# Seven-product feed-forward: one PSUM tile per partial sum, products in an order that a small list scheduler writes, weight parts six products ahead

## The chip, the cores and the metric

The kernel runs on one core of a Trainium2 chip. The metric is device time in microseconds (us) of one execution. TensorE (PE in the rows, its weight loads PEld) multiplies, VectorE (DVE) and ScalarE (ACT) prepare operands and drain PSUM, SyncE (SP) issues the weight loads. Before the change the time is 3714.63 us, the median of three runs (3712.78 to 3716.22).

## The reference: what is computed

Two models run one after the other on 512 tokens of width 1024. The second is a two-layer network on 528 tokens (512 and 16 meta tokens), each layer a feed-forward, a mixer and another feed-forward. The change touches only the second model's four feed-forwards:

```
def swiglu(x, w_gate, w_up, w_down):
    return (jax.nn.silu(x @ w_gate) * (x @ w_up)) @ w_down

h = h + 0.5 * swiglu(rmsnorm(h, norm_gains[l, 0]), ffn_w_gate[l, 0], ffn_w_up[l, 0], ffn_w_down[l, 0])
h = h + mixer(...)
h = h + 0.5 * swiglu(rmsnorm(h, norm_gains[l, 2]), ffn_w_gate[l, 1], ffn_w_up[l, 1], ffn_w_down[l, 1])
```

`w_gate` and `w_up` are 1024 x 2816, `w_down` is 2816 x 1024, all float32. The last feed-forward drops the meta tokens and works on 512.

## The kernel before, in words

**Operands in two parts.** Each float32 operand is split into a high part (ScalarE copy to the rounded type, `whi`) and a low part (VectorE subtraction, `wlo`), in `wsplit` (L212 to L214) and `split` (L216). A product is then three matmuls: high by high, high by low, low by high. Weights come in pieces of 128 x 512 (`raw`, loaded by SyncE at L197 or L1016). The tiles rotate through a fixed number of buffers, `WB` at L51: 6 raw, 3 sum, 9 whi, 9 wlo. These rings serve the whole kernel.

**One feed-forward** (`ffn2`, L1087) has 22 hidden blocks of 128 columns. Block `m` needs a gate and an up column block. Seven of the blocks (`DIRECT`, L53: 0, 3, 7, 11, 15, 18, 21) are done directly: 48 matmuls into one PSUM tile for gate, 48 for up. The others are done as a pair by seven half-size products in place of eight (`strassen`, L1051): gate weights have halves `a`, `b` along the contraction, up weights `c`, `d`; the tokens have halves `a`, `b`. The parts are `a`, `b`, `d` and four sums s1 = c + d, s2 = s1 - a, s3 = a - c, s4 = b - s2 (`pair`, L1007). On the token side `form` (L317) makes two matching combinations, `f1` and `f2`, from four pairs of row blocks. A product (`prod`, L1041) is 12 matmuls of 264 columns (256 in the last feed-forward). The first feed-forward does blocks 0 to 2 directly, so that there are 13 + 3 x 15 = 58 pairs in all.

**PSUM.** In this part of the kernel a pool `psP` has three tiles of two banks each and `psS` two tiles of one bank. A pair takes one `psP` tile `yx` that holds two sums, Y in its first bank and X in its second, and one tile `z`. Y is not cleared between products: `a`, `s2`, `s3`, `d` accumulate on it one after another, and it is copied out between them by ScalarE (L1064, L1069, L1075). X and Z are added by VectorE (L1062).

**The order.** The products of a pair go to TensorE as: `a`, `b` | `s2` | `s1`, `s3` | `d` | `s4`. The generator is stepped by hand (L1141 to L1147) so that the previous pair's `d` comes between `b` and `s2`, and its `s4` between `s2` and `s1`. TensorE keeps that order (`pinned`, L225). All seven parts of a pair are written ahead of the pair before it (`ahead`, L1124), as far as buffers let them. The framework's scheduler sets the order on the other engines at build time, earlier code first among what it holds ready; at run time each engine works through its own list in order.

**Rounds.** After blocks 7, 15 and 21 (`ROUNDS`, L52) the blocks so far are multiplied by their rows of `w_down`: eight outputs (`dn`), each a sum over the round's 8 or 6 blocks. `act` (L1112) makes a block's hidden value: scale, silu, product, split. Before that, at the start of a feed-forward, `stats` and `stats2` compute the norm factor `rb`, and `forms` the last of the token combinations.

Of the kernel before, what the change touches and what calls it, by code (L numbers as in the profile page):

```python
# [16 lines left out]
AF = mybir.ActivationFunctionType  # L17
# [43 lines left out]
class Net:  # L61
    def __init__(self, ctx, tc, d):
        nc = self.nc = tc.nc
        self.tc = tc
        self.d = d
        self.n = 0
        self.xp = ctx.enter_context(tc.tile_pool(name="xp", bufs=1))
        self.cp = ctx.enter_context(tc.tile_pool(name="cp", bufs=1))
        self.sp = ctx.enter_context(tc.tile_pool(name="sp", bufs=NSLOT))
        self.mp = ctx.enter_context(tc.tile_pool(name="mp", bufs=24))  # L70
        self.qp = ctx.enter_context(tc.tile_pool(name="qp", bufs=8))
        self.wp = ctx.enter_context(tc.tile_pool(name="wp", bufs=4))
# [5 lines left out]
        self.pinned = False  # L78

        self.cst = self.cp.tile([128, 144], F32, name="cst")  # L80
# [129 lines left out]
        return w[c // WU][:, c % WU : c % WU + n]  # L210

    def wsplit(self, raw, hi, lo, c):  # L212
        self.nc.scalar.activation(hi[:, c], raw[:, c], AF.Copy)  # L213
        self.nc.vector.tensor_tensor(out=lo[:, c], in0=raw[:, c], in1=hi[:, c], op=ALU.subtract)  # L214

    def split(self, a, name):  # L216
        nc = self.nc
# [786 lines left out]
    def c2(self, l, off):  # L1004
        return lambda k: self.v2[:, l * V2 + off + k : l * V2 + off + k + 1]

    def pair(self, gsrc, usrc):  # L1007


        nc = self.nc  # L1010
        C = slice(0, WU)
        raw = []
        for src in (gsrc, usrc):
            for h in range(2):
                raw.append(self.wtile("raw"))
                nc.sync.dma_start(raw[-1], src[:, WU * h : WU * h + WU])  # L1016
        a, b, c, d = raw

        def parts(t):
            h, l = self.wtile("whi"), self.wtile("wlo")  # L1020
            self.wsplit(t, h, l, C)
            return h, l

        def sum_(i, j, op=ALU.subtract):
            t = self.wtile("sum")
            nc.vector.tensor_tensor(out=t, in0=i, in1=j, op=op)
            return t

        w = {"a": parts(a), "b": parts(b)}
        s1 = sum_(c, d, ALU.add)  # L1030
        s2 = sum_(s1, a)
        w["s2"] = parts(s2)
        s3 = sum_(a, c)
        w["s1"] = parts(s1)
        s4 = sum_(b, s2)
        w["s3"] = parts(s3)
        w["d"] = parts(d)
        w["s4"] = parts(s4)
        return w

    def prod(self, o, w, xs, c, first):  # L1041

# [5 lines left out]
                    stop=k == NK // 2 - 1 and i == 2, skip_group_check=not first,  # L1048
                )

    def strassen(self, w, xs, T, rb, act):  # L1051


        nc = self.nc
        h = T // 2
        a, b = slice(0, h), slice(h, T)
        x1, x2 = xs[: NK // 2], xs[NK // 2 :]
        f1, f2 = zip(*self.forms)
        pa = self.P("yx")
# [3 lines left out]
        self.prod(Y, w["a"], x1, a, True)  # L1063
        nc.scalar.copy(s[:, a], Y)  # L1064
        self.prod(X, w["b"], x2, a, True)
        tt(s[:, a], X, s[:, a], ALU.add)
        yield
        self.prod(Y, w["s2"], f2, a, False)
        nc.scalar.copy(s[:, b], Y)  # L1069
        yield  # L1070
        pz = self.P("z")
        Z = pz[:, 0, :h]
        self.prod(Z, w["s1"], f1, a, True)
        self.prod(Y, w["s3"], f1, b, False)
        nc.scalar.copy(u[:, b], Y)  # L1075
        tt(u[:, b], Z, u[:, b], ALU.add)
        yield
        self.prod(Y, w["d"], f2, b, False)
        tt(u[:, b], u[:, b], rb[:, b], ALU.mult)
        tt(u[:, a], Y, rb[:, a], ALU.mult)  # L1080
        yield
        self.prod(Z, w["s4"], x2, b, False)
        tt(s[:, b], Z, s[:, b], ALU.add)
        act(s, u, True)
        yield

    def ffn2(self, l, f, xs, g, next_g, out=None):  # L1087
        nc, d = self.nc, self.d
        T = NX if (l, f) == (L - 1, 1) else T2
        self.psum(2)  # L1090
        gw, uw, dw = d["ffn_g"][l, f], d["ffn_u"][l, f], d["ffn_d"][l, f]
        acts = []
        srcs = [w for m in range(NF) for w in (gw[m], uw[m])]
        done = []
        if (l, f) == (0, 0):
# [13 lines left out]
                    nc.scalar.copy(t[:, :T], p[1])  # L1109
                    done.append(t[:, :T])  # L1110

        def act(s, u, scale):  # L1112
# [4 lines left out]
            acts.append(self.split(s[:, :T], "fa"))  # L1117

        pend = iter(())
        new = []  # L1120
        seven = lambda m: m < NF and not (m in DIRECT or done[2 * m : 2 * m + 2])
        wp = {}

        def ahead(m):  # L1124

            if m not in wp and seven(m):
                wp[m] = self.pair(srcs[2 * m], srcs[2 * m + 1])

        def forms():
            for k in range(len(self.forms), NK // 2):  # L1130
                self.form(k, T, g)

        if done:
            forms()
        for m in range(NF):
            ahead(m)
            self.pinned = m > 0
            if seven(m):
                if seven(m + 1) and m + 1 not in ROUNDS:
                    ahead(m + 1)  # L1140
                cur = self.strassen(wp.pop(m), xs, T, rb, act)  # L1141
                next(cur)
                next(pend, None)
                next(cur)
                next(pend, None)
                next(cur)
                pend = cur  # L1147
            else:
                ps = done[2 * m : 2 * m + 2]
                o = 2 * m + len(ps)  # L1150
                if m == 0 and not ps:
# [5 lines left out]
                for i in range(o, 2 * m + 2):  # L1157
                    if len(ps) == 2:
                        break
                    p = self.outs(1, T, "gu")  # L1160
                    self.group([srcs[i]], xs, T, p)
                    ps.append(p[0][1])
                    for _ in pend:
                        pass
                act(self.mul_r(ps[0], rb, "fg"), self.mul_r(ps[1], rb, "fu"), False)
            if m + 1 in ROUNDS:
                for _ in pend:
                    pass
                o = m + 1 - len(acts)
                fin = m == NF - 1  # L1170
                if fin:
                    self.forms = self.next_forms
                dsrc = lambda i: dw[i][:, 128 * o : 128 * m + 128]
                for i in range(NK - 1 if fin and out is not None else NK):
                    p = self.outs(1, T, "dn")[0]
                    self.down(dsrc(i), acts, T, p)
                    xv = self.xt[i][:, :T]
                    nc.vector.scalar_tensor_tensor(
                        out=xv, in0=p[1], scalar=0.5, in1=xv, op0=ALU.mult, op1=ALU.add
                    )  # L1180
                    if fin:
                        new.append(self.finish(i, T, next_g))
                if fin and out is not None:
                    self.ending(out, self.wload(dsrc(NK - 1)), acts)
                acts.clear()
        self.pinned = False
        return new

    def ending(self, out, ws, acts):
# [776 lines left out]
```

## Time and profile before

| what | value |
|---|---|
| median of three runs | 3714.63 us |
| profiled execution, its own time | 3718.47 us |
| span of its instructions | 3716.7 us |
| TensorE matmul busy | 3544.7 us, 95% |
| weight load busy | 3146.8 us, 85% |
| VectorE busy | 2423.9 us, 65% |
| ScalarE busy | 1720.5 us, 46% |
| granted TensorE clock, mean | 0.986 |
| DMA, mean | 82 GB/s |

The trace covers 3716.7 of the 3718.47 us of its execution; the remaining 1.8 us lie around the span. Busy time counts a matmul from its start to its modelled end, so successive matmuls overlap: one of 264 columns lasts 0.28 us and the next starts 0.12 us later. Time is therefore counted below from start to start. A row of a window gives its bounds and length, then the busy us and the count of PE, PEld, DVE, ACT and POOL, the granted clock (1.00 is 2.4 GHz, 0.50 is 1.2 GHz), the DMA share and GB/s. A bracket behind a timeline row gives the idle time of the engine before that instruction and what ended it.

### The profile page before, as it was taken

To read this page: it belongs to the slowest core of one execution; us is meant where nothing else is said; L and a number is where in the kernel's file an instruction comes from. 1 tells how busy PE (TensorE), PEld (TensorE's weight loads), DVE (VectorE), ACT (ScalarE), POOL (GpSimd) and SP (SyncE) were. 2 spreads that over 40 slices of the span, in tenths; PEclk is the share of its full clock that TensorE was granted. 3 is DMA by queue.
4 is the path that set the end of the run, shared out by engine and by line. 5 is a ranking of instruction groups with operands and counts; after the bars stand their busy time and mean duration, and the time that the engine had idled before them with its cause. 6 is when DMAs were issued, how large, how long until landed. Compare 5 with 4: busy or idle time off the path is not lost. (4 is left out here: it accounts for less than half of the span.)

```text
span 3716.7 us, 60666 instructions
## 1 busy us (share of the span) xinstructions
PE 3544.7 (95%) x23303; PEld 3146.8 (85%) x23303; DVE 2423.9 (65%) x4863; ACT 1720.5 (46%) x3219; POOL 44.3 (1%) x184
## 2 busy tenths in 40 slices
PE   8999999999999899999999999998999999989998
PEld 6778888678888799998989999998999987778887
DVE  6778744777763767566546667576666664677765
ACT  3655434365543434344673444344334557444432
POOL 1000000000000000000000000000000000000000
PEclk9999999999999999999999999999999999999998
DMA  4213333212333223231121232323233212223232
GB/s 142 69 55 104 95 93 104 76 48 89 95 93 94 74 85 90 86 99 55 55 61 58 75 97 81 93 83 87 85 92 92 73 55 69 60 75 108 79 96 65
DMA packets 170178, 305.02 MB, mean 82 GB/s; under 512 B 19460, under 2 KB 29732, under 8 KB 169888
## 3 DMA queue, kind: packets, MB, share of 16 engines
q1 hardware_dynamic: 165888, 292.89, 26.7%
q0 software_dynamic: 2560, 6.93, 0.5%
q8 instruction: 183, 3.00, 0.3%
q10 hardware_dynamic: 1440, 1.32, 0.1%
q14 instruction: 107, 0.88, 0.1%
HBM read 298.97 MB, written 2.10 MB: 81 GB/s over the span
## 5 line engine op out<-in xcount | busy, mean ns | idle before, releaser
L213 ACT ACTIVATE whi<-raw 128x512 fp32r<-128x512 f32 (+1 forms) x1078 | 664.1, 619 | 1115.4 <-PE dn L227 359.4
L214 DVE TENSOR_TENSOR wlo<-raw,whi 128x512 fp32r<-128x512 f32 (+1 forms) x1078 | 723.5, 673 | 445.2 <-ACT whi L213 426.5
L227 PE MATMUL g<-xh,whi 128*128 128x256 f32 (+4 forms) x1192 | 332.2, 335 | 9.8 <-ACT xh L292 5.9
L227 PE MATMUL g<-xl,whi 128*128 128x256 f32 (+4 forms) x1192 | 318.0, 321 | 0.3 <-DVE xl L293 0.3
L227 PE MATMUL g<-xh,wlo 128*128 128x256 f32 (+4 forms) x1192 | 314.4, 319 | 0.0
L227 PE MATMUL up<-xh,wlo 128*128 128x512 f32 (+1 forms) x768 | 289.3, 377 | 0.0
L227 PE MATMUL up<-xl,whi 128*128 128x512 f32 (+1 forms) x768 | 289.0, 377 | 0.1
L227 PE MATMUL up<-xh,whi 128*128 128x512 f32 (+1 forms) x768 | 288.3, 377 | 0.0
L227 PE MATMUL dn<-fah,wlo 128*128 128x256 f32 (+1 forms) x1238 | 285.3, 300 | 0.0
L227 PE MATMUL dn<-fah,whi 128*128 128x256 f32 (+1 forms) x1238 | 285.2, 300 | 0.0
L227 PE MATMUL dn<-fal,whi 128*128 128x256 f32 (+1 forms) x1238 | 284.8, 299 | 0.0
L213 ACT ACTIVATE whi<-sum 128x512 fp32r<-128x512 f32 x232 | 146.5, 632 | 274.4 <-PE yx L227 129.5
L227 PEld LDWEIGHTS g<-xh,whi 128*128 128x128 f32 (+1 forms) x1192 | 198.4, 189 | 45.1 <-issue 15.8
L227 PE MATMUL yx<-xh,whi 128*128 128x264 f32 (+1 forms) x464 | 139.3, 300 | 81.5 <-ACT fg L1064 81.5
L227 PEld LDWEIGHTS g<-xl,whi 128*128 128x128 f32 (+1 forms) x1192 | 200.6, 188 | 15.5 <-issue 2.6
L227 PEld LDWEIGHTS g<-xh,wlo 128*128 128x128 f32 (+1 forms) x1192 | 199.9, 188 | 14.9
L227 PE MATMUL gu<-xh,whi 128*128 128x256 f32 (+2 forms) x848 | 197.7, 302 | 14.6 <-DVE fg L423 12.1
L214 DVE TENSOR_TENSOR wlo<-sum,whi 128x512 fp32r<-128x512 f32 x232 | 159.8, 689 | 71.8 <-ACT whi L213 66.8
L227 PEld LDWEIGHTS dn<-fah,whi 128*128 128x128 f32 x1238 | 200.3, 189 | 7.4
L227 PEld LDWEIGHTS dn<-fal,whi 128*128 128x128 f32 x1238 | 200.1, 189 | 7.5
L227 PEld LDWEIGHTS dn<-fah,wlo 128*128 128x128 f32 x1238 | 199.9, 188 | 7.4
L227 PE MATMUL gu<-xl,whi 128*128 128x256 f32 (+2 forms) x848 | 198.2, 301 | 0.7 <-DVE xl L293 0.7
(496 smaller groups left out, 8514.0 us busy)
## 6 DMA issues: line engine op xcount, KB each, us to landing
raw<-w_in SPq DMA_DIRECT2D x186, 256.0 KB, 2.8
raw<-w_up SPq DMA_DIRECT2D x176, 256.0 KB, 2.9
raw<-ffn_g SPq DMA_DIRECT2D x176, 256.0 KB, 2.8
raw<-ffn_u SPq DMA_DIRECT2D x176, 256.0 KB, 2.9
raw<-ffn_d SPq DMA_DIRECT2D x160, 256.0 KB, 2.7
raw<-w_down SPq DMA_DIRECT2D x80, 256.0 KB, 2.7
raw<-w_out SPq DMA_DIRECT2D x64, 256.0 KB, 2.7
raw<-w_pab SPq DMA_DIRECT2D x32, 256.0 KB, 2.7
```

The lines of the kernel that those rows point to most:

```text
L213: self.nc.scalar.activation(hi[:, c], raw[:, c], AF.Copy)
L214: self.nc.vector.tensor_tensor(out=lo[:, c], in0=raw[:, c], in1=hi[:, c], op=ALU.subtract)
L227: i = self.nc.tensor.matmul(*a, **k)
```

## The change

Y gets a `psP` tile of its own (one bank used) and X a one-bank tile from `psS`. The hand-stepped generator becomes a table of seven functions p1 (`a`), p2 (`b`), p6 (`s2`), p5 (`s1`), p7 (`s3`), p4 (`d`), p3 (`s4`), and the direct blocks become two, g and u. `product_order` writes one list of them for a round. It counts in matmuls (12 a product, 48 a direct half), lets at most two blocks be open, at most three `psP` tiles be held, and counts 24 from the end of a product to the use of what it leaves. Weight parts are written, in the same order, six entries ahead of their product, and `queue` orders the loads and the three kinds of part among themselves. The rings become 6 raw, 5 sum, 8 whi, 8 wlo. The blocks that precede the list (0, or 0 to 2 in the first feed-forward) come ahead of `forms`; before, in the first feed-forward, `forms` came first. The down products are no longer pinned.

```
-WB = {"raw": 6, "sum": 3, "whi": 9, "wlo": 9}
+WB = {"raw": 6, "sum": 5, "whi": 8, "wlo": 8}
+LEAD = 6
+USES = {"p1": ("a",), "p2": ("b",), "p6": ("s2",), "p5": ("s1",), "p7": ("s3",), "p4": ("d",), "p3": ("s4",), "g": "ab", "u": "cd"}
...
+    def queue(self, key, i):
+        if key in self.last:
+            self.tc.add_manual_dep(
+                i.ins, self.last[key], mybir.DependencyInfo(mybir.DependencyClass.NoSync, mybir.DependencyReason.DATA),
+                reason="queue",
+            )
+        self.last[key] = i.ins.name
...
-    def pair(self, gsrc, usrc):
+    def parts_of(self, gsrc, usrc):
+        t = {}
+        def get(n):
+            if n in t:
+                return t[n]
+            if n in "abcd":
+                h = slice(WU * (n in "bd"), WU * (n in "bd") + WU)
+                t[n] = self.wtile("raw")
+                self.queue("raw", nc.sync.dma_start(t[n], (gsrc if n in "ab" else usrc)[:, h]))
+            else:
+                i, j = {"s1": "cd", "s2": ("s1", "a"), "s3": "ac", "s4": ("b", "s2")}[n]
+                i, j = get(i), get(j)
+                t[n] = self.wtile("sum")
+                op = ALU.add if n == "s1" else ALU.subtract
+                self.queue("sum", nc.vector.tensor_tensor(out=t[n], in0=i, in1=j, op=op))
+            return t[n]
+        def parts(n):
             h, l = self.wtile("whi"), self.wtile("wlo")
+            ih, il = self.wsplit(get(n), h, l, slice(0, WU))
+            self.queue("whi", ih)
+            self.queue("wlo", il)
             return h, l
...
-    def strassen(self, w, xs, T, rb, act):
+    def strassen(self, i, xs, T, rb, act):
...
-        pa = self.P("yx")
-        Y, X = pa[:, 0, :h], pa[:, 1, :h]
...
+        def p1(w):
+            Y = ps["Y"] = self.P("y")[:, 0, :h]
+            self.prod(Y, w[0], x1, a, True)
+            nc.scalar.copy(s[:, a], Y)
+        def p2(w):
+            X = self.S("x")[:, :h]
+            self.prod(X, w[0], x2, a, True)
+            tt(s[:, a], X, s[:, a], ALU.add)
...
+    def product_order(kinds):
+        LAT = 24
+        need = {"p6": ("p1",), "p5": ("p1",), "p7": ("p6", "p5"), "p4": ("p7",), "p3": ("p7",), "p2": ("p1",)}
+        takes, frees = {"p1", "p5", "g", "u"}, {"p4", "p3", "g", "u"}
...
+            for m, o in left:
+                if m > first + 1:
+                    break
+                at = max([t] + [end[m, d] + (0 if (d, o) in (("p1", "p2"), ("p1", "p5"), ("p5", "p7")) else LAT) for d in need.get(o, ()) if (m, d) in end])
...
+                if best is None or at < best[0]:
+                    best = (at, m, o)
...
+            order = self.product_order(["7" if seven(m) else "2" for m in ms])
+            for n in range(len(order) + LEAD):
+                if n < len(order):
+                    i, o = order[n]
+                    if i not in get:
+                        get[i] = self.parts_of(srcs[2 * ms[i]], srcs[2 * ms[i] + 1])
+                    w[i, o] = [get[i](p) for p in USES[o]]
+                if n >= LEAD:
+                    i, o = order[n - LEAD]
...
+                    do[i][o](w.pop((i, o)))
+            self.pinned = False
```

The function's answer for the blocks 8 to 15 (the number is the block, a direct block has g and u):

```
8.p1 8.p2 8.p5 8.p6 9.p1 9.p2 8.p7 9.p6 8.p4 8.p3 9.p5 9.p7 10.p1 10.p2 9.p4 9.p3 10.p6 10.p5 11.g 10.p7 11.u 10.p4 10.p3
12.p1 12.p2 12.p5 12.p6 13.p1 13.p2 12.p7 13.p6 12.p4 12.p3 13.p5 13.p7 14.p1 14.p2 13.p4 13.p3 14.p6 14.p5 15.g 14.p7 15.u 14.p4 14.p3
```

Blocks 0 to 7 end in the same way (7.u 6.p4 6.p3); blocks 16 to 21 end in 21.g 20.p4 20.p3 21.u. At 58 entries over the four feed-forwards the function itself counts a wait, of 12 matmuls each, 23 times at a p4 (8.p4), 23 times at a p5 (9.p5) and 12 times at a u (11.u).

## Rows read from the trace of the kernel before

**Rows 1.** Waits of PE, whole span: engine, line, releaser: us in total, times, longest.
```profile
PE yx L227 <- ACT fg L1064: 81.5, 58, 8.0
PE yx L227 <- DVE fg L1062: 13.7, 23, 0.6
PE gu L227 <- DVE fg L423: 12.1, 1, 12.1
...
PE bc L394 <- DVE rs_y L381: 7.3, 4, 2.8
```

**Rows 2.** Timeline of all engines, block 5's first two products.
```profile
1321.63 0.28 PE L227 MATMUL yx<-xh,wlo 128*128 128x264 f32 x1
...
1322.41 0.36 ACT L1064 COPY fg<-yx 128x264 f32<-128x264 f32 x1
...
1322.83 0.39 PE L227 MATMUL yx<-xh,whi 128*128 128x264 f32 x1 [0.91 <-ACT fg L1064]
```

**Rows 3.** Busy time by window: round 8 to 15; sum of all twelve rounds.
```profile
1404.49:1498.92 94.43, 86.96 (x698) 85.28 (x697) 72.02 (x121) 45.14 (x83) 0.00 (x0) 1.00 0.33 95
...
sum 1011.86, PE 899.68 PEld 868.35 DVE 727.94 ACT 462.99 POOL 2.83; mean PE 74.97 PEld 72.36 DVE 60.66 ACT 38.58 POOL 0.24
```

**Rows 4.** The same for unbroken work: three products, a direct half; both widths.
```profile
1417.93:1422.34 4.41, 4.41 (x39) 4.41 (x38) 2.92 (x5) 2.16 (x4) 0.00 (x0) 1.00 0.27 95
1436.75:1442.59 5.84, 5.84 (x51) 5.84 (x49) 5.14 (x10) 2.29 (x5) 0.00 (x0) 1.00 0.28 93
3606.13:3610.35 4.22, 4.22 (x38) 4.22 (x37) 2.85 (x6) 2.16 (x4) 0.00 (x0) 1.00 0.41 138
3613.18:3618.73 5.55, 5.55 (x26) 4.52 (x25) 5.05 (x9) 2.21 (x5) 0.00 (x0) 1.00 0.31 94
```

**Rows 5.** Timeline of PE, first pair of the second, third and fourth feed-forward.
```profile
2108.87 0.28 PE L227 MATMUL yx<-xh,wlo 128*128 128x264 f32 x1
2115.79 0.59 PE L227 MATMUL yx<-xh,whi 128*128 128x264 f32 x1 [6.64 <-ACT fg L1064]
...
2520.17 0.59 PE L227 MATMUL yx<-xh,whi 128*128 128x264 f32 x1 [7.33 <-ACT fg L1064]
...
3331.07 0.58 PE L227 MATMUL yx<-xh,whi 128*128 128x256 f32 x1 [7.96 <-ACT fg L1064]
```

**Rows 6.** Timeline of ACT at the first of these.
```profile
2112.12 1.28 ACT L1115 ACT_TABLE_LOAD   x1 [1.81 <-DVE fg L423]
...
2115.38 0.36 ACT L1064 COPY fg<-yx 128x264 f32<-128x264 f32 x1
```

**Rows 7.** Timeline of DVE, first feed-forward: end of the combinations, draining of block 2.
```profile
1293.34 0.70 DVE L222 TENSOR_TENSOR fvl<-tv,fvh 128x528 fp32r<-128x528 f32 x1
...
1300.89 0.70 DVE L423 TENSOR_TENSOR fg<-gu,rbc 128x528 f32<-128x528 f32 x1
```

**Rows 8.** Timeline of DVE, instructions back to back, two places.
```profile
1427.40 0.43 DVE L1062 TENSOR_TENSOR fu<-z,fu 128x264 f32<-128x264 f32 x1
1427.74 0.68 DVE L214 TENSOR_TENSOR wlo<-raw,whi 128x512 fp32r<-128x512 f32 x1
...
1436.70 0.68 DVE L214 TENSOR_TENSOR wlo<-raw,whi 128x512 fp32r<-128x512 f32 x1
1437.30 0.70 DVE L1116 TENSOR_TENSOR fg<-fg,fu 128x528 f32<-128x528 f32 x1
1437.92 0.68 DVE L214 TENSOR_TENSOR wlo<-sum,whi 128x512 fp32r<-128x512 f32 x1
```

**Rows 9.** Waits of DVE for a weight load, whole span.
```profile
DVE sum L1026 <- DMA raw<-ffn_u: 12.6, 15, 2.4
```

**Rows 10.** DMA issues of the page: count, KB each, us to landing.
```profile
raw<-ffn_u SPq DMA_DIRECT2D x176, 256.0 KB, 2.9
```

**Rows 11.** Timeline of PE and DVE, a pair's last product to its split.
```profile
1340.18 0.28 PE L227 MATMUL z<-xh,wlo 128*128 128x264 f32 x1
...
1344.64 0.70 DVE L222 TENSOR_TENSOR fal<-fg,fah 128x528 fp32r<-128x528 f32 x1
```

More of the change, by code (lines that the diff above doesn't have):

```diff
@@ L78, in __init__ @@
         self.pinned = False
+        self.last = {}
         self.cst = self.cp.tile([128, 144], F32, name="cst")
@@ L1005, in c2 @@
         return lambda k: self.v2[:, l * V2 + off + k : l * V2 + off + k + 1]
-    def pair(self, gsrc, usrc):
+    def parts_of(self, gsrc, usrc):
         nc = self.nc
[L1011 to L1019, printed above, removed]
+        t = {}
[14 more added lines that the diff above has]
+        def parts(n):
             h, l = self.wtile("whi"), self.wtile("wlo")
-            self.wsplit(t, h, l, C)
+            ih, il = self.wsplit(get(n), h, l, slice(0, WU))
+            self.queue("whi", ih)
+            self.queue("wlo", il)
             return h, l
[L1024 to L1039, printed above, removed]
+        return parts
     def prod(self, o, w, xs, c, first):
@@ L1049, in prod, with whole, one, go @@
                 )
-    def strassen(self, w, xs, T, rb, act):
+    def whole(self, i, xs, T, rb, act):
+        ps = {}
+        def one(o):
+            def go(w):
+                p = self.outs(1, T, "gu")[0]
+                w = tuple(zip(*w))
+                for k in range(NK):
+                    self.mm3(p[0], w, k * 128, xs[k], T, k == 0, k == NK - 1)
+                ps[o] = self.mul_r(p[1], rb, "f" + o)
+                if o == "u":
+                    act(i, ps["g"], ps["u"], False)
+            return go
+        return {"g": one("g"), "u": one("u")}
+    def strassen(self, i, xs, T, rb, act):
         nc = self.nc
@@ L1070, in strassen @@
[L1070 to L1084, printed above, removed]
@@ L1085, in strassen, with p6, p5 @@
-        yield
+        ps = {}
+        def p1(w):
[6 more added lines that the diff above has]
+            tt(s[:, a], X, s[:, a], ALU.add)
+        def p6(w):
+            self.prod(ps["Y"], w[0], f2, a, False)
+            nc.scalar.copy(s[:, b], ps["Y"])
+        def p5(w):
+            Z = ps["Z"] = self.P("z")[:, 0, :h]
+            self.prod(Z, w[0], f1, a, True)
@@ new lines, in p7, with p4, p3 @@
+        def p7(w):
+            self.prod(ps["Y"], w[0], f1, b, False)
+            nc.scalar.copy(u[:, b], ps["Y"])
+            tt(u[:, b], ps["Z"], u[:, b], ALU.add)
+        def p4(w):
+            self.prod(ps["Y"], w[0], f2, b, False)
+            tt(u[:, b], u[:, b], rb[:, b], ALU.mult)
+            tt(u[:, a], ps["Y"], rb[:, a], ALU.mult)
+        def p3(w):
+            self.prod(ps["Z"], w[0], x2, b, False)
+            tt(s[:, b], ps["Z"], s[:, b], ALU.add)
+            act(i, s, u, True)
@@ new lines, in strassen @@
+        return {"p1": p1, "p2": p2, "p6": p6, "p5": p5, "p7": p7, "p4": p4, "p3": p3}
+    @staticmethod
+    def product_order(kinds):
+        LAT = 24
+        need = {"p6": ("p1",), "p5": ("p1",), "p7": ("p6", "p5"), "p4": ("p7",), "p3": ("p7",), "p2": ("p1",)}
+        takes, frees = {"p1", "p5", "g", "u"}, {"p4", "p3", "g", "u"}
+        left = [(m, o) for m, kd in enumerate(kinds) for o in (("p1", "p2", "p6", "p5", "p7", "p4", "p3") if kd == "7" else ("g", "u"))]
+        end, out, t = {}, [], 0
+        hold = []
+        while left:
+            first = left[0][0]
+            best = None
+            for m, o in left:
+                if m > first + 1:
+                    break
+                at = max([t] + [end[m, d] + (0 if (d, o) in (("p1", "p2"), ("p1", "p5"), ("p5", "p7")) else LAT) for d in need.get(o, ()) if (m, d) in end])
+                if any((m, d) not in end for d in need.get(o, ())):
+                    continue
+                if o in takes:
+                    busy = [f for f in hold if f is None or f > t]
+                    if len(busy) >= 3:
+                        if None in busy and sum(f is None for f in busy) >= 3:
+                            continue
+                        at = max(at, sorted(f for f in busy if f is not None)[len(busy) - 3])
+                if best is None or at < best[0]:
+                    best = (at, m, o)
+            at, m, o = best
+            t = at + (48 if o in ("g", "u") else 12)
+            end[m, o] = t
+            left.remove((m, o))
+            if o in takes:
+                hold = [f for f in hold if f is None or f > at]
+                hold.append(t + LAT if o in ("g", "u") else None)
+            elif o in frees:
+                hold.remove(None)
+                hold.append(t + LAT)
+            out.append((m, o))
+        return out
@@ L1110, in ffn2, with act @@
                     done.append(t[:, :T])
-        def act(s, u, scale):
+        def act(i, s, u, scale):
             if scale:
@@ L1116, in act @@
             nc.vector.tensor_tensor(out=s[:, :T], in0=s[:, :T], in1=u[:, :T], op=ALU.mult)
-            acts.append(self.split(s[:, :T], "fa"))
-        pend = iter(())
+            acts[i] = self.split(s[:, :T], "fa")
         new = []
[L1121 to L1127, printed above, removed]
-        def forms():
[L1130 to L1148, printed above, removed]
+        seven = lambda m: not (m in DIRECT or done[2 * m : 2 * m + 2])
+        def forms():
+            while len(self.forms) < NK // 2:
+                self.form(len(self.forms), T, g)
+        m0 = 0
+        for m1 in ROUNDS:
+            ms = list(range(m0, m1))
+            for m in ms[: 1 if not m0 and not done else (NR + 1) // 2 if not m0 else 0]:
                 ps = done[2 * m : 2 * m + 2]
-                o = 2 * m + len(ps)
-                if m == 0 and not ps:
+                if not ps:
                     ps = self.outs(2, T, "gu")
@@ L1156, in ffn2 @@
                     ps = [p[1] for p in ps]
-                for i in range(o, 2 * m + 2):
-                    if len(ps) == 2:
-                        break
+                elif len(ps) == 1:
                     p = self.outs(1, T, "gu")
[L1161 to L1170, printed above, removed]
-                if fin:
[L1172 to L1185, printed above, removed]
@@ L1186, in ffn2 @@
-        self.pinned = False
+                    self.group([srcs[2 * m + 1]], xs, T, p)
+                    ps = ps + [p[0][1]]
+                act(m, self.mul_r(ps[0], rb, "fg"), self.mul_r(ps[1], rb, "fu"), False)
+                ms = ms[1:]
+            forms()
+            self.pinned = True
+            get, w, do = {}, {}, {}
+            order = self.product_order(["7" if seven(m) else "2" for m in ms])
[7 more added lines that the diff above has]
+                    i, o = order[n - LEAD]
+                    m = ms[i]
+                    if i not in do:
+                        f = self.strassen if seven(m) else self.whole
+                        do[i] = f(m - m0, xs, T, rb, act)
+                    do[i][o](w.pop((i, o)))
@@ new lines, in ffn2 @@
+            self.pinned = False
+            fin = m1 == NF
+            if fin:
+                self.forms = self.next_forms
+            dsrc = lambda i: dw[i][:, 128 * m0 : 128 * m1]
+            for i in range(NK - 1 if fin and out is not None else NK):
+                p = self.outs(1, T, "dn")[0]
+                self.down(dsrc(i), acts, T, p)
+                xv = self.xt[i][:, :T]
+                nc.vector.scalar_tensor_tensor(out=xv, in0=p[1], scalar=0.5, in1=xv, op0=ALU.mult, op1=ALU.add)
+                if fin:
+                    new.append(self.finish(i, T, next_g))
@@ L1187, in ffn2 @@
+            if fin and out is not None:
+                self.ending(out, self.wload(dsrc(NK - 1)), acts)
+            acts.clear()
+            m0 = m1
         return new
```

14 lines of the change are left out of this document (4 added, 10 removed).

## The prediction

> **What bounds the kernel now.** I read the page first: TensorE is busy 95% of the span and the chain that ended last is almost all TensorE, so only its waits and its low-clock time can be won. Then its waits. The first line of that view is the whole case: the first matmul of X waits for ScalarE's copy of Y (L1064) 58 times, once in each pair, 81.5 us in all; 23 times, in the first pair of a run, the product `s2` then waits for VectorE's reading of X (L1062), 13.7 us; one wait of 12.1 us belongs to the start of the first feed-forward [rows 1]. X and Y lie in different banks but in one tile, and each of these waits is an instruction on one of the two sums held until the other sum has been read. The timeline shows it closely: Y's last matmul starts at 1321.63, the copy at 1322.41 lasts 0.36, X's first starts at 1322.83; that is 1.20 us from start to start where 0.12 is the step [rows 2].
>
> Last I took windows, to see everything that the rounds lose and not only what the view of waits books. There are twelve rounds; from a round's first product to its first down product (in the first feed-forward from the second half of block 3 on) they take 1011.86 us together, 94.43 of them in round 8 to 15 [rows 3]. Unbroken, three products take 4.41 us, so 1.47 each, and a direct half 5.84; in the last feed-forward 4.22 / 3 = 1.407 and 5.55 [rows 4]. By the code those windows hold 301 products and 35 halves of 528 tokens and 105 products and 12 halves of 512: 442.5 + 204.4 + 147.7 + 66.6 = 861.2 us. So 1011.9 - 861.2 = **151 us** are waits, slow restarts and low clock. It is more than the waits' 107 because a matmul after a pause lasts 0.39 and not 0.28 [rows 2], and 0.59 after a long one [rows 5], twice the 0.28, which I read as the lower of the two clocks. 151 us is all that the change can win in the products; the down products between the rounds have no wait to lose.
>
> **The change, part by part.**
>
> *X in a tile of its own.* It adds no instruction. The 58 waits of X for the copy go, and the 23 of `s2` for X, with their restarts. What is late next? By the new order p1, p2, p5 follow each other and p6 needs the copy of Y two products, 2.9 us, after p1; the copy was done 1.2 us after it. No stall there, except at the heads (next).
>
> *Heads of the last three feed-forwards.* There the copy itself is late: X waits 6.64, 7.33 and 7.96 us [rows 5], because ScalarE has block 0's silu, with a table load of 1.28, ahead of the copy in its list and starts the copy at 2115.38, 6.5 us after Y's last matmul [rows 5, 6]. Nothing in the change moves that. Two products, p2 and p5, now lie inside the wait and p6 takes what is left: 6.64 - 2.9 = 3.7 and 7.96 - 2.8 = 5.1. In the second case the two fall into an earlier pause, the 2.8 us for the norm factor [rows 1], and the 7.33 stay. That is 16 us, and I add 2 us each for the low clock behind such a pause: **22 us stay**. Ends: 0, if the copy comes ahead of the silu in ScalarE's new list, and 30, if the pauses stay whole and the clock falls each time.
>
> *Head of the first feed-forward.* The 12.1 us arise because block 2's tile is drained at 1300.89, after three blocks' `act` that came behind four token combinations ending at 1293.34 [rows 1, 7]. Now the `act`s come first, and the combinations have until 4.p5: block 3 is 2 x 5.84 and 4.p1, 4.p2 are 2.9, so 14.6 us from the end of block 2. VectorE's load in that time is four combinations (each four instructions of half width and two of full width, in the steps of [rows 8] 4 x 0.34 + 2 x 0.62 = 2.6 us), eight parts at 0.60 and one `act` of three at 0.62, 17 us. I leave **6 us**: 4 of stall, 2 of clock; ends 0 and 12.
>
> *The new order.* The same 12 matmuls a product. Its planner itself counts 58 waits of 12 matmuls (1.47 us): it wants 24 matmuls, 2.9 us, from a product to the use of its sum and finds only one product to put between. If that were so, 58 x 1.47 = 85 us would come back. But what it waits for took 1.20 us from the last matmul's start to the restart [rows 2], less than the 1.47 of the one product between. An instruction of 0.6 on the draining engine can stand in front, which makes 1.8, so 0 to 0.63 each, 0 to 36 us. I take 0.1 each, **6 us**, near the row.
>
> *The down products.* Rounds 0 to 7 and 8 to 15 now end with a pair's last product and no longer with a direct half. From its last matmul to the end of its split it takes 1344.64 + 0.70 - 1340.18 = 5.2 us [rows 11]; the down product reaches this block as its seventh, after 6 x 6 matmuls of 0.12, 4.4 us. Eight rounds at 0 to 0.8, **3 us**. Losing the pin costs nothing: TensorE has nothing else to do there.
>
> *Parts six ahead.* Six products are 8.8 us. The parts of a pair are as many as before: 7 splits and 4 sums on VectorE, five half-width additions and three of full width. In steps from start to start these are 0.60, 0.34 and 0.62 [rows 8]: 11 x 0.60 + 5 x 0.34 + 3 x 0.62 = 10.2 us against 7 x 1.47 = 10.3 of TensorE. That is tight in a run of two or three pairs, but VectorE was busy 72 of 94 us in a round that has direct blocks as well [rows 3], and they give it time. VectorE can be held up by a load: 15 waits of 0.84 on average for `c` or `d` before [rows 9]. If each of 58 pairs had one and nothing covered it, 49 us; with 8.8 us of lead I take **4 us**.
>
> *Rings 9 to 8.* They serve the other stages too. The view of TensorE's waits has no line for a weight part, which is the end at 0; the other end is the longest wait for a load, 2.4 us [rows 9], in each of the six other stages, 14. I take **3 us**.
>
> A rule of the Trainium skill speaks against the parts' sum. The page "VectorE: DVE Perf Modes", section "The DRAIN you can't avoid", says that a VectorE instruction does not start until the pipe of the one before has emptied, so that full durations would add. By that rule a pair's VectorE work is 11 x 0.68 + 5 x 0.43 + 3 x 0.70 = 11.7 us, over the 10.3 of its products, and VectorE would set the pace in every run of pairs. The trace disagrees: a split of 0.68 us is followed by the next instruction 0.60 us after its start, a half-width addition of 0.43 after 0.34 [rows 8]. The rule is kept as a rival below.
>
> *Sum.* 151 - 22 - 6 - 6 - 3 - 4 - 3 = **107 us** won. The trace's execution took 3718.5, so 3611; that execution lies 3.8 above the median of the runs, so **3608 us**.
>
> **The rivals.**
>
> 1. *The planner's waits are real in part.* A drain behind a split in ScalarE's or VectorE's list makes half of the 58 x 1.47, 43 us: 3650. For it: both engines work in list order and VectorE is nearly full in a run. Against: the 1.20 us.
> 2. *VectorE's durations add up.* (11.7 - 10.3) x 58 = 84 us back: 3692. For it: 72 us busy of 94 already. Against: the steps of 0.60.
> 3. *The loads come late: slower.* A pair holds four of six raw buffers, and the next pair's `c` and `d` can be loaded only when `a` and `c` have served s3. From there it is 2.9 us to landing [rows 10] and four steps of 0.6, 5.4 us, of the 8.8 that the lead gives; the loads, sums and splits are chained in one order, so one late load holds all behind it. Where more than 3.4 us are lost on the way TensorE stalls, and from 151 / 58 = 2.6 us a pair the change is a loss. With a landing uncovered in each pair it is 58 x 2.9 = 168 us: 151 won, 168 lost, 3732. Against: the same six buffers gave TensorE no wait before.
> 4. *The wait was not the tile's.* X waits for the copy all the same, and it stays at 3715. Against: 58 of 58 end just behind the copy, 23 of 23 behind X's reading.
> 5. *Everything goes*, heads included: 3718.5 - 151 - 3.8 = 3564.
>
> **How the numbers follow.** Forecast 0.64, with its own range 3590 to 3630; rival 1 0.14, rival 2 0.05, rival 3 0.05, rival 4 0.03, rival 5 0.09. The range 3575 to 3668 takes in the forecast, most of rival 1 and half of rival 5: 0.8. The ends of the terms added up would keep 141 of the 151 us, but they are six independent ones. A measurement of this kernel tells 0.2%, 7.4 us, from no change. Faster are the forecast and rivals 1, 2 and 5: 0.91 with some off for their tails; same rival 4 and those tails, 0.04; slower rival 3, 0.05.
>
> **What would show it.** In the changed kernel's waits the line of X for L1064 is gone, and no other line of TensorE in the feed-forwards is over 30 us. The twelve rounds take 890 to 915 us. The largest waits left are three of 4 to 8 us, of p6 for the copy of Y, at the heads. VectorE's busy time is as before, 2424 us, over a shorter span. Wrong would be: a wait of the products for `wlo` or `whi` (rivals 2 and 3), long waits of VectorE's sums for a load (rival 3), many waits of y for copies with 0.5 us or more (rival 1), or gaps opened in the other stages.

## The result, and the profile after

The changed kernel takes **3613.89 us** (median of four runs, 3611.3 to 3618.5); the kernel before took 3715.43 beside it (3712.8 to 3717.9). The ratio is 0.9728, 95% interval [0.9711, 0.9745]: 101.5 us faster. The forecast was 3608, its range 3575 to 3668. The profiled execution took 3618.50 us, its span 3616.4, at a mean granted clock of 0.988. Of all executions reported below one stands apart: one of eight of the version with X back in Y's tile took 6956.9 us at a granted clock of 1.00, for no cause that its record shows; without it that version's median would be 3704.8 in place of 3705.4.

First the waits of TensorE in the changed kernel, the five longest (engine, line, releaser: us in total, times, longest; lines have moved: L1093 is the copy of Y that was L1064, L436 the reading of a direct block's tile that was L423):

```profile
PE z L231 <- DVE fg L436: 17.6, 4, 9.3
PE ssq L355 <- DVE acc L319: 9.4, 3, 5.4
PE y L231 <- ACT fg L1093: 7.9, 7, 1.6
PE ssy L355 <- DVE acc L319: 7.1, 4, 1.9
PE bc L407 <- DVE rs_y L394: 7.0, 4, 3.2
```

The 58 and the 23 waits of [rows 1] are gone, 95.2 us. In their place is something that [rows 1] does not have: Z, the tile of p5, waits four times for VectorE. The busy times of the changed kernel's page:

```profile
PE 3526.4 (98%) x23303; PEld 3141.2 (87%) x23303; DVE 2405.9 (67%) x4863; ACT 1718.5 (48%) x3219; POOL 44.4 (1%) x184
```

The same place as [rows 2], block 5's first two products, in the timeline of the changed kernel:

```profile
1319.16 0.28 PE L231 MATMUL y<-xh,wlo 128*128 128x264 f32 x1
1319.28 0.28 PE L231 MATMUL x<-xh,whi 128*128 128x264 f32 x1
...
1319.94 0.36 ACT L1093 COPY fg<-y 128x264 f32<-128x264 f32 x1
```

X's first matmul starts 0.12 us behind Y's last, where it was 1.20, and the copy reads Y while X is being written. The Trainium skill, page "PSUM — Partial Sum Buffer", section "Summary: rules for kernel authors", asks for this: a read beside a running matmul should have a different bank, or at least a different quadrant. The trace agrees as far as it goes: the 0.36 us copy lies under matmuls at the 0.12 step, and no run here reads the bank that a matmul is writing. But the kernel before already had two banks; what it lacked was two tiles.

The twelve rounds of the changed kernel, the answer to [rows 3] (bounds and length; busy us and count of PE, PEld, DVE, ACT, POOL; clock, DMA share, GB/s). Shown are the first round of each feed-forward, round 8 to 15 and 16 to 21 of the first, and the sum of all twelve:

```profile
1294.58:1354.32 59.74, 50.46 (x399) 50.27 (x397) 46.51 (x84) 29.97 (x55) 0.00 (x0) 0.91 0.28 81
1401.34:1487.44 86.10, 84.96 (x699) 84.75 (x697) 68.77 (x118) 44.67 (x82) 0.00 (x0) 1.00 0.35 99
1534.37:1599.08 64.71, 64.69 (x530) 64.30 (x529) 47.37 (x82) 31.58 (x59) 1.41 (x7) 1.00 0.35 100
2089.57:2167.96 78.39, 75.33 (x615) 74.74 (x614) 62.02 (x109) 41.76 (x75) 0.00 (x0) 1.00 0.32 96
...
2461.29:2549.40 88.11, 80.63 (x624) 79.58 (x623) 65.56 (x121) 41.77 (x77) 0.00 (x0) 0.94 0.32 94
...
3249.15:3331.88 82.73, 77.62 (x526) 72.42 (x525) 62.13 (x112) 42.14 (x77) 0.00 (x0) 0.94 0.31 91
...
sum 905.41, PE 875.84 PEld 859.28 DVE 698.69 ACT 460.23 POOL 2.83; mean PE 72.99 PEld 71.61 DVE 58.22 ACT 38.35 POOL 0.24
```

1011.86 - 905.41 = **106.45 us** came from the rounds, and 905.4 - 861.2 = 44 us of excess over unbroken work are left. Where they lie can be seen from the rows: rounds 16 to 21 are full (64.69 busy of 64.71), rounds 8 to 15 lose about one us each (1.8 in the last feed-forward), and the first rounds of the feed-forwards lose the rest, two of them at a clock of 0.94 and one at 0.91. The two profiled executions differ by 100.0 us, so 6.4 were lost outside the rounds; the section on the prediction comes back to them.

What the first rounds wait for is seen at the third feed-forward's start (timeline of the changed kernel, ACT, DVE and PE, in order of time; a bracket gives the engine's idle time and what ended it):

```profile
2466.07 1.48 PE L407 MATMUL bc<-cst,rs_y 128*128 128x128 f32 x10 [3.17 <-DVE rs_y L394]
2467.27 0.66 ACT L430 COPY rbc<-bc 128x512 f32<-128x512 f32 x2 [3.77 <-PE bc L407]
2467.82 0.53 ACT L341 ACTIVATE tt<-xt,v 128x264 f32<-128x264 f32 x1
...
2468.38 0.49 DVE L338 SCALAR_TENSOR_TENSOR tu<-xt,v,tt 128x264 f32<-128x264 f32 x1 [2.36 <-ACT tt L341]
...
2470.78 0.63 ACT L216 ACTIVATE whi<-sum 128x512 fp32r<-128x512 f32 x1 [2.44 <-issue]
2471.32 0.63 ACT L225 ACTIVATE fuh<-tu 128x528 fp32r<-128x528 f32 x1
...
2472.67 0.70 DVE L226 TENSOR_TENSOR fvl<-tv,fvh 128x528 fp32r<-128x528 f32 x1
2473.29 0.70 DVE L436 TENSOR_TENSOR fg<-gu,rbc 128x528 f32<-128x528 f32 x1
...
2474.04 0.39 PE L231 MATMUL z<-fuh,whi 128*128 128x264 f32 x1 [3.13 <-DVE fg L436]
...
2477.13 0.36 ACT L1093 COPY fg<-y 128x264 f32<-128x264 f32 x1
...
2477.54 0.59 PE L231 MATMUL y<-fvh,whi 128*128 128x264 f32 x1 [0.83 <-ACT fg L1093]
```

p5 needs a `psP` tile. There are three: Y has one, block 0's gate and up have the other two. VectorE could free the gate tile from about 2468 on, when the norm factor is copied, but has the last token combination ahead of it in its list, which itself begins only after a ScalarE instruction that stands behind that copy. So `fg`, the copy-out of the gate tile, starts at 2473.29 and p5 at 2474.04. In this feed-forward part of the delay is ScalarE's: the combination's split `fuh` stands behind a weight part (`whi` of a sum) before which ScalarE is idle for 2.44 us. The profile names no releaser for that idle time, so its cause is not shown; at the other two heads it is not there.

### The profile page after: what moved, and what is told of

Same layout as the page of the kernel before. It is cut to its first block, busy times and chain, and to the rows that moved or that the text cites. A ratio compares the mean times of both kernels' runs of the same rounds, so it can differ in the third digit from the quotient of the medians.

```text
span 3616.4 us, 60587 instructions
## 1 busy us (share of the span) xinstructions
PE 3526.4 (98%) x23303; PEld 3141.2 (87%) x23303; DVE 2405.9 (67%) x4863; ACT 1718.5 (48%) x3219; POOL 44.4 (1%) x184
## 4 chain that ended last, share of the span: by engine, by line
PE 75%; DVE 3%; ACT 2%; issue 1%; DMA 0%; DVEq 0%; ACTq 0%; SPq 0%
PE dn L231 17%; PE g L231 12%; PE y L231 9%; PE gu L231 9%; PE up L231 7%; PE z L231 5%; PE wo L231 3%; PE x L231 2%; PE pb L231 1%; PE pa L231 1%; PE oa L1503 1%; PE sc L1469 1%; PE go L1733 1%; PE ptr L1486 1%; PE pvd L582 1%
## 5 line engine op out<-in xcount | busy, mean ns | idle before, releaser
L231 PE MATMUL gu<-xh,wlo 128*128 128x256 f32 (+2 forms) x848 | 197.6, 299 | 0.0
```

## Experiments

Each row is the median, and the ratio to the kernel before, measured beside it, with its 95% interval.

| kernel | us | ratio |
|---|---|---|
| changed kernel, again | 3613.0 | 0.9725 [0.971, 0.9739] |
| tile split alone | 3623.6 | 0.9749 [0.9735, 0.9764] |
| changed, X back in Y's tile | 3705.4 | 0.997 [0.9959, 0.9981] |
| changed, combinations ahead of block 0 | 3604.1 | 0.9698 [0.9681, 0.9714] |
| the same, again | 3603.1 | 0.9696 [0.968, 0.9713] |
| tile split, combinations ahead of block 0 | 3612.4 | 0.9716 [0.97, 0.9732] |
| changed, combinations ahead, order of before | 3611.3 | 0.972 [0.9706, 0.9735] |
| changed, pair after pair | 3744.7 | 1.0077 [1.0062, 1.0092] |
| changed, pair after pair, p5 ahead of p6 | 3759.5 | 1.0112 [1.0092, 1.0133] |
| changed, parts two ahead | 3613.4 | 0.9723 [0.9708, 0.9737] |
| changed, 116 more sums on VectorE | 3634.2 | 0.9779 [0.9764, 0.9794] |

**The changed kernel once more.**

> The changed kernel once more, as the yardstick of the runs beside it. All theories: 3611 to 3619 us. If the 3.8 us that the profiled execution lost before the first feed-forward, in a stretch of low granted clock, belong to that execution alone, its first down product of the second block is back at the time that it has in the kernel before, within 1 us; if the shorter rings of weight parts cost them, they are there again.

3613.0 us (3610.7 to 3621.1), with 17.3 us of waits of Z and 7.9 of y for the copy: the profile repeats.

**The tile split alone**, in the kernel before:

```diff
-        pa = self.P("yx")
-        Y, X = pa[:, 0, :h], pa[:, 1, :h]
+        Y, X = self.P("y")[:, 0, :h], self.S("x")[:, :h]
```

> The kernel before with one edit: Y and X in tiles of their own; hand-stepped order, weight parts and rings as before. Theory T (the wait for the copy belongs to the shared tile, and that alone holds the gain): the 58 waits of X and the 23 of s2 are gone, the twelve rounds lose 95 to 100 us of their 151, the head of the first feed-forward keeps its 12 us: 3615 to 3630. Rival O (the order by the planner and the lead of six hold half of it): the waits move to p6, p7 and p4, 0.5 to 0.9 us a pair, 3650 to 3670.

3716.9 - 3623.6 = 93.3 us with one line, of the 103.9 that the whole change won beside it. Its waits of TensorE:

```profile
PE y L227 <- ACT fg L1063: 19.4, 7, 7.4
PE gu L227 <- DVE fg L423: 12.1, 1, 12.1
```

The 12.1 of [rows 1] stand as they were. Of the 19.4 the late copy at the last three heads is 18.7 (5.18, 6.11 and 7.44 us), where it was 21.9 [rows 5].

**The split undone** in the changed kernel:

```diff
-            Y = ps["Y"] = self.P("y")[:, 0, :h]
+            pa = self.P("yx")
+            Y, ps["X"] = pa[:, 0, :h], pa[:, 1, :h]
+            ps["Y"] = Y
...
-            X = self.S("x")[:, :h]
+            X = ps["X"]
```

> The changed kernel with one edit undone: X again in the second bank of Y's tile; order, parts and rings stay new. Theory T: p2 follows p1 directly and waits for the copy in each pair, 58 times 0.9 us and a restart of 0.15 to 0.2: 62 us back, 3672 to 3685. Rival O: the new order hides it, 3614 to 3640.

3705.4: more than expected came back, 92.4 us. The waits of TensorE, and one of them in the timeline:

```profile
PE yx L231 <- ACT fg L1095: 101.0, 58, 12.2
```

```profile
1452.11 0.39 PE L231 MATMUL yx<-xh,whi 128*128 128x264 f32 x1 [3.54 <-ACT fg L1095]
```

Of the 58, 43 cost 0.91 to 0.93 (31 before); after a direct block the copy stands behind other work of ScalarE and the 11 waits cost 1.5 to 3.54, at the four heads 5.6 to 12.2. That is why more came back than the 62 us expected. So the tile is worth 92 to 93 us from either side. Without it the new order and the rest are worth 11.5 us (3705.4 against 3716.9), with it 10.6 (3613.0 against 3623.6).

**The combinations ahead of block 0.** This tests the reading of the heads. The combinations are written before block 0 (in the first feed-forward before block 3), so that VectorE frees the tiles without them in the way:

```diff
+                if len(done) == NR - 1:
+                    forms()
...
-                    rb = self.group(srcs[:2], xs, T, ps, r=r)
                     forms()
+                    rb = self.group(srcs[:2], xs, T, ps, r=r)
```

> The changed kernel with the token combinations written ahead of the first weight group (in the first feed-forward after four of its five direct halves), so that they lie ahead of the norm factor and of the drains in the lists of ScalarE and VectorE. Theory H (at the heads p5 waits for block 0's PSUM tile, whose drain lies behind the last combination, and that one behind the copy of the norm factor): the 17.6 us of p5 fall below 8 and the four heads give 10 to 18 us, 3597 to 3606. Rival V (VectorE is full at the heads, and the order of its work moves the wait without making it smaller): 3611 to 3618, with the wait under another name.

> The version with the token combinations ahead of block 0, once more beside the one with the order of before: 3602 to 3607.

3604.1 and 3603.1, the fastest here, 9 to 10 us under the changed kernel. Its longest waits of TensorE:

```profile
PE bc L407 <- DVE rs_y L394: 10.3, 5, 3.6
PE gu L231 <- DVE fg L436: 9.5, 1, 9.5
...
PE y L231 <- ACT fg L1093: 9.5, 7, 2.9
```

The wait of Z is gone. In the last three feed-forwards the time from the first direct matmul to the first down product falls from 289.58 to 280.28, which is the whole gain; in the first it does not (75.35 from the norm factor on, 74.97 in the changed kernel). There the 9.3 of Z came back as 9.5 of block 3's tile, with VectorE busy 22.7 of the 25.0 us before it (1275 to 1300). So the three later heads were a matter of VectorE's list, as theory H has it, and the first one of its load, as rival V has it.

**Split and early combinations, and the order of before.** The first kernel has the tile split and the early combinations, nothing else of the change. The second has the whole change and the early combinations, but its list of products is that of before:

```diff
-            order = self.product_order(["7" if seven(m) else "2" for m in ms])
+            order, last = [], []
+            for i, m in enumerate(ms):
+                if seven(m):
+                    order += [(i, "p1"), (i, "p2")] + last[:1] + [(i, "p6")] + last[1:] + [(i, "p5"), (i, "p7")]
+                    last = [(i, "p4"), (i, "p3")]
+                else:
+                    order += [(i, "g")] + last + [(i, "u")]
+                    last = []
```

> The kernel before, hand-stepped, with separate tiles for Y and X and the token combinations ahead of the first weight group. Theory I (the hand-stepped order is as good as the planner's inside the runs; the planner's 10 us over it lie at the heads): the combinations give 8 to 14 us here as well, 3608 to 3616, and a round of blocks 8 to 15 takes 85.3 us, under the 86.1 of the changed kernel. Rival O (the planner's order is worth 10 us everywhere): 3614 to 3625.

> The version with the token combinations ahead of block 0 (3604.1), its products in the order of the kernel before (p1 p2 | last p4 | p6 | last p3 | p5 p7) in place of the planner's. Theory: in the runs the order of before is the better by 0.8 us in each round 8 to 15 (85.28 against 86.10), at the heads the planner's p5 ahead of p6 was worth the 8 us between 3612.4 and 3604.1: the time is 3608 to 3614. Rival: those 8 us lay elsewhere in the new writing of parts and rings; then the order costs nothing at the heads and this version takes 3599 to 3603.

3612.4 and 3611.3. These two differ in the writing of parts, the rings, the queues and the pin of the down products: together 1 us, no change that can be told. The second differs from the version at 3603.1 by the order alone, 8 us. The round 8 to 15 of the first feed-forward in the second of them:

```profile
1402.86:1488.03 85.17, 85.12 (x698) 84.91 (x697) 70.15 (x121) 45.15 (x83) 0.00 (x0) 1.00 0.33 104
```

85.17 against 86.10: within this round the old order is the better one. The planner's puts `12.p6` where ScalarE has the `act` of blocks 10 and 11 ahead of the copy, and waits 1.1 us. It wins elsewhere. Against the version that took 3603.1 beside it, the stretch named above is 285.90 us (93.97 + 96.94 + 94.99) in the last three feed-forwards with the order of before and 278.58 with the planner's, 7.3 us; the four rounds 16 to 21 are 258.59 and 254.85, 3.7 us; the four rounds 8 to 15 are 337.05 and 341.44 and give 4.4 back. That is 6.7 of the 7.1 us between the two spans. The sums over that stretch of the last three feed-forwards, with the order of before and with the planner's:

```profile
sum 285.90, PE 270.71 PEld 261.77 DVE 227.67 ACT 146.28 POOL 0.00; mean PE 90.24 PEld 87.26 DVE 75.89 ACT 48.76 POOL 0.00
sum 278.58, PE 266.75 PEld 258.19 DVE 222.95 ACT 143.24 POOL 0.00; mean PE 88.92 PEld 86.06 DVE 74.32 ACT 47.75 POOL 0.00
```

**Pair after pair**, without the planner, and then with p5 ahead of p6:

```diff
-            order = self.product_order(["7" if seven(m) else "2" for m in ms])
+            order = [(i, o) for i, m in enumerate(ms) for o in (("p1", "p2", "p6", "p5", "p7", "p4", "p3") if seven(m) else ("g", "u"))]
```

> The changed kernel without the planner: each block's products one after another (p1 p2 p6 p5 p7 p4 p3, then the next block), separate tiles, parts and lead in that order. Theory I (any order that puts one product between a sum and its next use will do, the hand-stepped one as well, and only adjacency costs): p4 follows p7 directly and waits for the copy of Y, 1.1 us and a restart of 0.15 in each of 58 pairs, 70 us back: 3675 to 3695. Rival N (with separate tiles the order does not matter): 3610 to 3630.

> Pair after pair as in the plain order (3744.7), but in each pair p5 comes ahead of p6. Theory: the plain order lost by p6 (39 waits, 77.8 us), because the copy of Y stands behind the previous block's act in ScalarE's list and ends about 2.9 us after p1, while one product (1.47) lay between; now two lie between, 2.9 us. The waits of 1.46 go, the waits of p4 for its sum behind p7 (58, 52.1 us) stay: 3744.7 - 39 x 1.46 = 3688, range 3675 to 3700. Rival: the plain order loses because drains of one pair crowd together whatever comes first; then p5 or p7 waits instead, and the time stays at 3720 to 3745.

3744.7 and 3759.5 (3746.1 to 3763.4): 0.8% and 1.1% above the kernel before, and both expectations were wrong. The waits of TensorE, first the plain order:

```profile
PE y L231 <- ACT fg L1093: 77.8, 39, 11.3
PE y L231 <- ACT fu L1110: 52.1, 58, 1.2
```

and with p5 ahead of p6:

```profile
PE y L231 <- ACT fg L1102: 53.3, 58, 0.9
PE y L231 <- ACT fu L1110: 52.1, 58, 1.2
PE z L231 <- DVE fg L436: 19.2, 4, 9.1
```

p4 comes right behind p7 on the same Y and waits 0.9 us on average for the copy between them, 58 times; that was expected. In the first kernel p6, which has one product between it and p1, waits as well, 39 times, which was not. The timeline of one of these places, in the first kernel:

```profile
1420.69 0.65 ACT L1193 ACTIVATE fg<-fg 128x528 f32<-128x528 f32 x1
1421.66 0.63 ACT L216 ACTIVATE whi<-sum 128x512 fp32r<-128x512 f32 x1 [0.32 <-PE x L231]
1422.19 0.63 ACT L225 ACTIVATE fah<-fg 128x528 fp32r<-128x528 f32 x1
...
1422.73 0.36 ACT L1093 COPY fg<-y 128x264 f32<-128x264 f32 x1
1423.14 0.39 PE L231 MATMUL y<-fvh,whi 128*128 128x264 f32 x1 [1.46 <-ACT fg L1093]
```

The previous block's silu and split and a weight part stand ahead of the copy in ScalarE's list. With p5 ahead, p6 waits three times and 3.0 us in all where it waited 39 times and 77.8, as the theory had it; but p7 is then right behind p6, and I had overlooked that this costs what p4 costs, 58 times 0.92, and p5 meets the late tiles of the heads again, 19.2. The profile of the second kernel is of its fastest execution, 3746.1; the other three took 3756 to 3763, and what they lost more is not shown. So a product that goes on with a sum right behind the product whose result must first be copied out costs 0.9 us in both places, and one product between is enough only when nothing stands before the copy.

**Parts two ahead.**

```diff
-LEAD = 6
+LEAD = 2
```

> The changed kernel with weight parts written two entries ahead instead of six. Theory B (buffers, not the lead, limit how early a part is made; the lead only ranks it): 3605 to 3625, the waits of products unchanged. Rival L (the lead is what covers load, sums and splits, 5.4 us, and two products are 2.9): 2.5 us in each pair, 145 us back, above 3700.

3613.4: no change. In this kernel the lead was not what keeps the parts ahead.

**More work for VectorE.** The sums s1 and s2 are computed twice, 116 instructions:

```diff
-                self.queue("sum", nc.vector.tensor_tensor(out=t[n], in0=i, in1=j, op=op))
+                for _ in range(2 if n in ("s1", "s2") else 1):
+                    self.queue("sum", nc.vector.tensor_tensor(out=t[n], in0=i, in1=j, op=op))
```

> The changed kernel with the sums s1 and s2 computed twice: two more VectorE instructions of 0.60 us a pair, 58 x 1.2 = 70 us of VectorE work, the outputs the same. Theory S (VectorE has slack in the runs because direct blocks and down products give its time back, and only at the four heads is it full): 0 to 8 us, at the heads, 3611 to 3622. Rival V (VectorE sets the pace of the runs, 10.2 of 10.3 us a pair): from half of the 70 us on, 3650 to 3685, with the products waiting for parts.

3634.2, 20.3 us more than the changed kernel, between the two theories. Where it lies, by windows of this kernel: round 8 to 15 and 16 to 21 of the first feed-forward, then:

```profile
1406.95:1493.37 86.42, 84.96 (x699) 84.75 (x697) 72.70 (x126) 44.49 (x82) 0.00 (x0) 1.00 0.33 99
1540.30:1604.54 64.24, 64.24 (x530) 64.22 (x529) 49.57 (x86) 32.00 (x59) 1.42 (x7) 1.00 0.33 100
```

```profile
2077.65:2177.41 99.76, 94.20 (x731) 92.39 (x729) 78.63 (x147) 47.41 (x86) 0.00 (x0) 0.95 0.30 88
2457.61:2563.03 105.42, 95.94 (x730) 94.21 (x729) 83.14 (x154) 48.40 (x90) 0.00 (x0) 0.92 0.28 84
3251.61:3349.27 97.66, 89.76 (x581) 82.45 (x580) 78.31 (x147) 46.69 (x85) 0.00 (x0) 0.93 0.30 90
sum 302.84, PE 279.90 PEld 269.05 DVE 240.09 ACT 142.50 POOL 0.00; mean PE 93.30 PEld 89.68 DVE 80.03 ACT 47.50 POOL 0.00
```

The later rounds stay at 86.42 and 64.24 against 86.10 and 64.71. The last three feed-forwards' beginnings (first direct matmul to first down product) take 302.84 where the changed kernel takes 289.58, 13.3 us more, and the first one 77.69 from the norm factor on against 74.97, 2.7 more: 16.0 of the 18.6 us between the spans. The four rounds 8 to 15 take 2.1 us more together (86.42, 86.48, 86.49 and 84.12 against 86.10, 86.18, 86.07 and 83.06), the rounds 16 to 21 nothing that can be told. So VectorE decides at the heads, and hardly in the rounds.

## Why the prediction was right

**The terms.** Of the 151 us, 41 were to stay in the rounds and 3 more to be lost in the other stages: 107 won. In the rounds 44.2 stayed, so 106.45 were won there, and 6.4 were lost outside: 100.0 between the two profiled executions, 101.5 between the medians. The mechanism, the shared tile, is shown. That the whole came so close is in part luck, because the smaller terms erred in both directions.

- *X in a tile of its own*: as forecast. The 58 and 23 waits are gone, and the tile alone is 92 to 93 us, shown by putting it in and by taking it out. Rival 4 is refuted.
- *Heads of the last three feed-forwards*: 22 us forecast, 28.2 measured (excess of those three rounds over unbroken work: 3.6, 13.3, 11.3). **The step failed in its place.** I had p6 wait 4 to 8 us for the copy of Y. p6 waits 0.83 to 1.58 there; ahead of it p5 waits 1.5 to 3.7 for a `psP` tile. Both together are 11.6 of the 28.2, where 16 were forecast for p6; the wait for the norm factor inside the third feed-forward's round is 3.5, and 81 matmuls that start over 0.18 us apart cost 8.6 more than at the full step, where 6 were forecast for the clock. I had counted PSUM tiles for the planner's list and not for the blocks that precede it, whose tiles VectorE frees behind the combinations. The early combinations took the wait away.
- *Head of the first feed-forward*: 6 forecast, 11.3 measured: a wait of 9.28 and about 2.0 of slow matmuls behind it (20 of them 0.22 apart and not 0.12). The race was the right one, VectorE's combinations and parts against 14.6 us of products, but what ends it is not the combination alone: block 3's tile is read after it. And VectorE's load was sized too small: from the end of block 2, about 1288.7 (two halves of 5.84 us before 4.p1 at 1300.42), to that reading at 1311.93 it works some 23 us where 17 were counted. Twelve parts lie there and not eight, five full-width steps of `act` and not three, and a combination takes 2.8 to 3.4 us and not 2.6, since three of its four half-width instructions are followed at 0.40 to 0.53 us where I had taken 0.34.
- *New order, down products, parts late*: 6 + 3 + 4 = 13 forecast, 4.8 measured, in rounds 8 to 15 and there mostly one late p6 each. None of the 58 waits that the planner counts occurs: the 1.20 us from sum to use is less than the 1.47 of a product, as I took it. (The upper end was worked out wrongly: 1.8 - 1.47 is 0.33 each and not 0.63, 19 us and not 36; with that the six ends add up to some 131 us and not 141. In rival 3, 2.9 us and four steps of 0.6 are 5.3 and not 5.4. The forecast hangs on none of these.) The down products start without a wait. Rival 1 falls.
- *Rings*: 3 us in the other stages, not shown. Kernels with equal orders and different rings are 1 us apart (3612.4 and 3611.3).

**Rival 2** (VectorE's durations add up) needed 84 us back; the rounds gave none of it, and 116 more instructions of 0.69 us cost a round 8 to 15 0.3 to 0.4 us, and 1.1 in the last feed-forward. The section of the Trainium skill that I set against the trace ("VectorE: DVE Perf Modes", "The DRAIN you can't avoid") ends its first paragraph with an exception that I did not weigh: an instruction that is not held starts earlier. The steps of [rows 8] agree with the exception. **Rival 3** (late loads): VectorE's sums did wait more for a load, 22.5 us in 23 waits against [rows 9], but no product waited for a part. **Rival 5** is excluded by the heads.

VectorE's busy time fell from 2423.9 to 2405.9 where I had it unchanged. The work is unchanged all the same: the durations of its 4863 instructions add up to 2615.9 us before and 2611.4 after, and busy time counts the overlap of successive instructions once, so that more of them now run back to back.

**What is left open.** The 6.4 us outside the rounds. 3.8 of them lie before the first feed-forward, where the change touches only the rings. The last down matmul of the first model starts at 1223.4 in the kernel before and at 1227.1 here; in the other single executions with the old rings it starts at 1225.9 and 1227.4, and in those with the new ones anywhere from 1222.6 to 1230.1. That is no order by rings; it looks like a difference between executions, and no run was made for it alone. For the other 2.6 us nothing is shown.

## What to carry to other kernels

A wait on a PSUM sum that nothing else shares is a wait on its tile: look first whether two sums in different banks lie in one tile, since here one line gave 93 of the 104 us measured beside it. Then ask of each product how far ahead its sum's reader is in ScalarE's or VectorE's list, not only how long that reader takes; 0.4 us of copy became 1.2 to 11 us of wait when other work stood before it. And count the tiles of a pool over the whole list, the hand-written beginning included, because after the inner waits are gone the beginning is where the time is left.

## What the runs showed beyond that

- After a pause TensorE is slow for a time that does not follow the length of the last pause: after one of 9.28 us the matmuls start 0.22 apart until 1317.3, 4.5 us at a granted clock of 0.50, the lower level; at the third feed-forward, after pauses of 3.17, 0.36, 3.13 and 0.83 us, they do so with one short break from 2467.9 to 2481.2, and the granted clock of 2461.29 to 2487.00 is 0.80.
- A planner's own count can be far off and its list good all the same: it counts 58 waits, the trace has none of them; it counts none at 12.p6, where the trace waits 1.1 to 1.2 us in each of the four rounds 8 to 15; and with the combinations ahead the order is still 8 us better than the one stepped by hand.
